# Heads and low-rank products by turns on the rows of the array, in a hybrid RWKV / retention / SSD / attention trunk

## The chip, the cores and the metric

The kernel runs on one core of a Trainium2 chip. The metric is device microseconds of that core for one execution of the whole program.

## The reference

Two layers (DEPTH = 2) of one trunk are applied to 128 context tokens and 512 latent tokens, width 1024, all in float32. Each layer norms its input, projects it into four groups of 256 channels (RWKV-7, retention, a state-space scan, differential attention), puts the four outputs through one projection, and then runs a gated convolutional feed-forward. The parts that the change touches are, in RWKV, the low-rank decay and gate, and in retention, the scores inside a chunk:

```
wd = wd.reshape(b, t, 2, 32); ad = ad.reshape(b, t, 2, 32)
w_lora = einsum('btdr,drc->btdc', tanh(wd), rwkv_w_up)
decay = exp(-exp(-softplus(-(rwkv_w0 + w_lora)) - 0.5))
a = sigmoid(rwkv_a0 + einsum('btdr,drc->btdc', ad, rwkv_a_up))
# RWKV state, per head of 64, both directions
S = S diag(w) + S (-kk)^T (kk * a) + v^T k;  o = S r
# retention, per head of 64 and chunk of 128
scores = einsum('bihd,bjhd->bijh', qc, kc) * decay
y = einsum('bijh,bjhe->bihe', scores, vc) + (qc * exp(cum)) S
```

## The kernel before

Channels lie on the partitions and tokens on the free axis: 512 latent columns, a zero column, 128 context columns (T = 642, STREAMS). All products are issued through one helper, mm, at line 84, so that the trace shows that line for nearly all of them and the tile names tell them apart. A product in plain float32 shows in the trace as two matmul records. Dense projections split their operands into two float32r parts and make three products each.

A Tile scheduler orders the instructions of an engine: an instruction that is ready early may stand ahead of one that comes earlier in the program, and program order is the priority among ready ones. PSUM is in two halves. The right one holds two pairs of banks for dense products. The left one (sbank, given out by SMT and XMT, in turn) holds four single banks during the RWKV scans, and three plus one for the modulation during retention.

**RWKV.** Each layer has four scans: two tiles t of two heads (64 channels each), two directions d. Scan i + 1 is prepared (rw_pre) beside the substitution of scan i (rw_sub) and the solve of scan i - 1 (the generator behind); the loops pump these generators a yield at a time, and the dense projections fill the rest. In rw_pre the inner function lora (line 524) makes tw, the decay, and ta, the gate: wa holds 128 rows, 32 for each of decay and gate in each direction. The weight tile wl [128, 4, 256] has in block g only the 32 rows of group g and zeros elsewhere, so that a product over all 128 rows picks one group. One call makes the products of 512 and of 128 columns (ztw or zta, line 530) with a Tanh on ACT behind each (line 532); tw is made whole, then ta. DVE then sums the decays (cum, line 550), and kd, AR and BK follow. The scores (sc) are made in three groups of 4, 4 and 2 chunks of 64 tokens (lines 590 to 597): for head 0 a bank is taken, 4 products of 64 rows are made and DVE multiplies the result by two masks (sca, pk); then the same for head 1. The substitution (xox, GU, xo) and the solve (bg, y, gq, st) take the same four banks.

**Retention.** It runs in an outer loop with the state-space scans, the modulation of what comes later (mps) and the projections that are left; each round takes one step of retention and of the state-space scans, 0.75 of modulation_behind and 0.5 of left(), whose last step is the value projection of the attention, dv (RS = (0.5, 0.0, 0.75, 1, 1, 1, 0.5)). The generator retention yields after kt and vw, then after each head (scores rsc into pt, in groups of 4 chunks and 1; qd on POOL), after three state steps (rin), after rin_c, after ryl and ryc with the squares, and in head_out (hs_ret, the statistics, and R_ret, their spread). The output goes to DRAM and is loaded again for the output projection. Two tiles t run one after the other.

**Derived.** Once a layer, wl is cleared on POOL (line 1312) and filled by four DMAs issued by ACT (line 1314).

Of the kernel before, what the change touches and what calls it, by code (L numbers as in the profile page):

```python
# [23 lines left out]
# token columns: latents 0..511, a zero column, context 513..640, a zero column  # L24
# [18 lines left out]
# columns of the per-layer parameter block  # L43
# [10 lines left out]
# columns of the constant block  # L54
# [17 lines left out]
def tile_trunk(ctx: ExitStack, tc: tile.TileContext, xT, cT, wmod, win, wv1, wv2, wout, wup, wdn, wlora, gup, pp, srw,  # L72
# [13 lines left out]
    class Pool:  # L86
        """A tile pool that can be closed out of turn; `bufs` per tag."""
# [14 lines left out]
    class Banks:  # L102
        """A half of PSUM: two pairs of banks (for the dense products) or four single banks."""
# [26 lines left out]
    def XMT(name):  # L130
        """a bank beside the dense products"""
        return sbank.tile(name)

# [23 lines left out]
    # silu(c) = u * (1 + tanh(u)), u = c / 2  # L157
# [30 lines left out]
    def w_pair(src, name):  # L188
        """the two halves (four blocks of the contraction each) of one column tile"""
        return [w_split(src[i], 512, f"{name}_{i}") for i in range(2)]  # L190
# [18 lines left out]
    def modulation(l, qs, bank=SMT, burst=False, pool=None):  # L209
        """in steps: one for each tile of weights, or (burst) for four of them"""  # L210
# [23 lines left out]
    def modulation_blocks(blocks, pool, n):  # L234
        """whole blocks, n tiles of weights loaded ahead"""
# [35 lines left out]
    def modulation_behind(l, qs, bank, pool, after):  # L271
        """loads, products and sums a step apart, each behind what runs beside it"""
# [42 lines left out]
    def spread(r, n, name, d, bank=SMT):  # L315
        """r [128 tokens, 5 * n]: rows of channels; n = 1 for all 128 channels, 2 for two heads of 64."""
# [12 lines left out]
    def x_stats(x, xp, name):  # L329
        """1/rms of x per token, spread over the partitions."""  # L330
# [21 lines left out]
    def norm(l, which, x, xp, name, before=None):  # L352
        """the stream h = rmsnorm(x) * g * (1 + scale) + shift, in two parts, zero columns between the streams"""
# [33 lines left out]
    def cm_product(parts, h, name, M=128):  # L387
        """[M channels, 2 halves of the tokens with one column of overlap on each side]"""
        hhi, hlo = h
        ps = MMT(name)  # L390
        for k in range(KD):
            wh, wl = wk(parts, k, M)
            for w_, r_, a, b in ((wh, hhi, k == 0, False), (wh, hlo, False, False), (wl, hhi, False, k == KD - 1)):
                for j, p0 in ((0, 0), (1, 321)):
                    mm(ps[:M, j, 0:324], lhsT=w_, rhs=r_[:, k, p0:p0 + 324], start=a, stop=b)
        return ps
# [4 lines left out]
    def tok_product(l, src, n, h, name, dest):  # L401
        """token rows of h @ W: dest [128 tokens, 5, n]"""
# [19 lines left out]
    def conv(ps, out, wl, wc, wr, bias=None, M=128):  # L422
        """centred taps along the tokens, from PSUM"""
# [10 lines left out]
    def head_stats(sqs, n, name, floor=None, scale=1.0 / 64, eps=EPS, bank=SMT, tg=""):  # L434
        """sqs: channel tiles [128, T] of squares -> per token and head, 1/sqrt, [128 tokens, 5 * n * len(sqs)]"""
# [8 lines left out]
    # mixer inputs and outputs wait in DRAM for their turn  # L444
# [18 lines left out]
    # ================= RWKV-7 =================  # L463
# [7 lines left out]
    def rw_proj(l, h, key, dv, out):  # L471
        """one projected tile, tokens shifted"""
# [11 lines left out]
    def rw_prep(l, t, f, dv, rw):  # L484
        """half normalised keys, and the values with tokens on partitions"""
# [10 lines left out]
    def rw_values(l, t, f, rw):  # L496
        """values with tokens on partitions: even chunks of 64 in the upper half, odd ones in the lower"""
# [18 lines left out]
    def rw_pre(l, t, d, f, wa, rw, dv, S, need):  # L516
        """up to the scores inside chunks and the right-hand sides"""
# [7 lines left out]
        def lora(base, bias, tag):  # L525
            out = RT(tag)[:, 0:T]
            pads(out)
            for c0, n in STREAMS:
                z = SMT(f"z{tag}{nm}_{c0}")
                mm(z[:, 0:n], lhsT=dv["wl"][:, base // 32, t * 128:t * 128 + 128], rhs=wa[:, c0:c0 + n],  # L530
                   start=True, stop=True)
                act(out[:, c0:c0 + n], z[:, 0:n], AF.Tanh, bias=dv[bias][:, td:td + 1], scale=0.5)
            return out

        tw = lora(32 * d, "w0h", "tw")
        ta = lora(64 + 32 * d, "a0h", "ta")
        yield
        # log decays, summed inside chunks of 64 with a leading (trailing) zero
# [40 lines left out]
        # scores inside chunks of 64, transposed: rows (b | k) of token j, columns (a | r) of token i  # L579
# [5 lines left out]
        for g, ms in enumerate(GRP):  # L585
# [4 lines left out]
            for h in range(2):  # L590
                ps = SMT(f"sc{nm}_{g}_{h}")
                for e in range(nb):
                    mm(ps[:, 128 * e:128 * e + 128], lhsT=B2[64 * h:64 * h + 64, n0 + e, :],
                       rhs=A4[64 * h:64 * h + 64, :, n0 + e, :], start=True, stop=True)
                p4 = ps[:, 0:128 * nb].rearrange("p (e s c) -> p e s c", e=nb, s=2)
                vtt(sca[:, h, n0:n0 + nb], p4[:, :, 0, :], maskA.unsqueeze(1).to_broadcast([128, nb, 64]), MULT)
                vtt(pk[:, 0:nb, h, 1, :], p4[:, :, 1, :], maskR.unsqueeze(1).to_broadcast([128, nb, 64]), MULT)
            # the strict blocks of 32 on the diagonal
# [12 lines left out]
        def rhs():  # L611
# [4 lines left out]
            for g, ms in enumerate(GRP):  # L616
# [7 lines left out]
                # right-hand sides [a | A_ak v], tokens on partitions, two chunks a pack  # L624
# [15 lines left out]
    def rw_sub(l, t, d, rw, dv, S):  # L640
        """inverses of the 16-blocks of I - A, transposed, by substitution"""
# [19 lines left out]
        # combined to blocks of 32: X1 O X2 beside the diagonal (X2 O X1 backwards)  # L661
# [21 lines left out]
        # and to blocks of 64: what lies beside the diagonal of the inverses is X1 O X2 again  # L683
# [6 lines left out]
        for e in range(2):  # L690
            # empty in this direction
# [24 lines left out]
    def rw_solve(l, t, d, f, rw, dv, y, S):  # L716
        """solve, the chunk maps, the states from chunk to chunk, the outputs"""
# [47 lines left out]
        # states from chunk to chunk; MI = [state (key, value) ; identity]  # L765
# [37 lines left out]
    def rw_end(l, t, f, rw, dv, y):  # L803
# [5 lines left out]
        # group norm over each head  # L809
# [19 lines left out]
    # ================= projections that wait =================  # L829
    def rope_tile(ps, out, tab, sp, nm):  # L830
        """rotary pairs lie 16 partitions apart in every 32; context columns turn by 0"""
# [8 lines left out]
    def silu2(ps, o):  # L840
        """2 * silu, from PSUM"""
# [43 lines left out]
    def diff_proj(l, h, sp):  # L885
        tab = sp.tile([128, 2, 660], tag="tab", name=f"dtab{l}")
        nc.scalar.dma_start(tab[:, :, 0:T], rope[1])
        # queries and keys in two exact parts, the cache behind the keys of the tokens
# [23 lines left out]
    def tokens_to_partitions(dst, src, nm):  # L912
        """dst [128 tokens, 5, 128] from src [128 channels, T]"""
# [6 lines left out]
    def head_out(l, nm, kk, y, sq, gcol, gate, bank=XMT, eps=EPS):  # L920
        """sq: the squares of y, then room"""
# [16 lines left out]
    # ================= retention =================  # L938
    def retention(l, t, mp, tokv, dv):
# [6 lines left out]
        # states entering each latent chunk: rows 0-63 forward, 64-127 backward  # L946
# [13 lines left out]
        # scores inside chunks of 128, transposed, times the decay of both directions  # L960
        pts, qds = [], []
        for h in range(2):
            rows = slice(64 * h, 64 * h + 64)
            pt = mp.tile([128, 5, 128], tag="pt", name=f"rpt{nm}_{h}")
            for n0, n1 in ((0, 4), (4, 5)):
                ps = XMT(f"rsc{nm}_{h}_{n0}")
                for n in range(n0, n1):
                    mm(ps[:, 128 * (n - n0):128 * (n - n0) + 128], lhsT=k[rows, TOK[n]:TOK[n] + 128],
                       rhs=q[rows, TOK[n]:TOK[n] + 128], start=True, stop=True)
                vtt(pt[:, n0:n1], ps[:, 0:128 * (n1 - n0)].rearrange("p (n i) -> p n i", i=128),  # L970
                    D4[:, h, t].unsqueeze(1).to_broadcast([128, n1 - n0, 128]), MULT)
            qd = mp.tile([128, 4, 128], tag="qd", name=f"qd{nm}_{h}")
# [3 lines left out]
            pts.append(pt)  # L976
            qds.append(qd)
            yield
# [40 lines left out]
    # ================= state-space duality =================  # L1019
    def ssd_dt(l, dtr, dv):  # L1020
        """dt = softplus, with log1p(e) = 2 atanh(e / (2 + e)); the decays that follow from it"""
# [24 lines left out]
        # sums of g: after j (forward) and before j (backward), and over the whole chunk  # L1046
# [854 lines left out]
```

## Time and profile before

| what | value |
|---|---|
| runs | 2264.86, 2267.35, 2267.46 us; median 2267.35 us |
| span of the profiled execution | 2266.46 us |
| PE, DVE, ACT, POOL busy | 94%, 58%, 36%, 12% |
| layer 0, RWKV scans | about 84 to 300 us |
| layer 0, retention | about 370 to 500 us |
| the same stages of layer 1 | some 1117 us later |

The profile is of one execution. PE is the engine of the matmuls, DVE the vector engine, ACT the scalar engine, POOL the third elementwise engine; the queues that issue DMAs are shown as SPq, ACTq, POOLq. A name such as ztw is the tile written; "ztw<-wa,wl" gives the tile and what it reads; a shape such as 32*128 128x512 is rows times columns of the array, then the output. Records of a pipelined matmul overlap, so the time from one start to the next start is what a product takes of PE, not its own duration. PEclk is the granted clock as a share of the full one.

### The profile page before, as it was taken

The numbers are of one execution on the slowest core, as the hardware profiler recorded it, in microseconds if no ns is written. First come the engines' busy times: TensorE is split into PE (matmuls) and PEld (weight loads), VectorE is DVE, ScalarE is ACT, GpSimd is POOL, SyncE is SP. The second block draws the span as 40 slices with busy tenths as digits, with TensorE's granted clock in tenths as the row PEclk, the third lists the DMA queues.
The fourth block names the chain that finished last, engine by engine and source line by source line (L and its number), as shares of the span: only waits on it lengthen the run. The fifth ranks groups of instructions, "written<-read, shape, count | busy, mean of one in ns | idle before, by whom it ended". The sixth has DMA issues, their size and how long they took to land. (4 is left out here: it accounts for less than half of the span.)

```text
span 2266.5 us, 41011 instructions
## 1 busy us (share of the span) xinstructions
PE 2136.9 (94%) x16265; PEld 1936.7 (85%) x16265; DVE 1307.2 (58%) x2951; ACT 816.4 (36%) x1603; POOL 275.2 (12%) x468
## 2 busy tenths in 40 slices
PE   6999999979999999999989999999799999999997
PEld 3887887767878899999988888777678899999997
DVE  3687776547564435545457777755475654454553
ACT  4343432226343313323344334332363432232332
POOL 3111122210020000000031111222001100000002
PEclk9999999988989999999999999999799999999998
DMA  6212126575233332222332211365832222222221
GB/s 241 77 55 67 49 80 226 181 213 137 68 94 121 123 87 71 71 79 75 92 89 60 72 51 56 98 221 176 235 102 73 75 75 71 75 73 77 73 72 67
DMA packets 130943, 232.26 MB, mean 102 GB/s; under 512 B 14784, under 2 KB 34752, under 8 KB 130752
## 3 DMA queue, kind: packets, MB, share of 16 engines
q1 hardware_dynamic: 98304, 176.47, 26.4%
q10 hardware_dynamic: 32448, 53.17, 7.2%
q8 instruction: 129, 2.11, 0.4%
q14 instruction: 62, 0.51, 0.1%
HBM read 199.16 MB, written 30.42 MB: 101 GB/s over the span
## 5 line engine op out<-in xcount | busy, mean ns | idle before, releaser
L84 PE MATMUL pu<-hhi_n,wh_up 128*128 128x324 f32 x1408 | 326.9, 314 | 0.6 <-DVE gv L426 0.6
L84 PE MATMUL pu<-hlo_n,wh_up 128*128 128x324 f32 x1408 | 325.9, 313 | 0.5 <-POOL hlo_n L381 0.4
L84 PE MATMUL pu<-hhi_n,wl_up 128*128 128x324 f32 x1408 | 324.5, 312 | 0.0
L185 DVE TENSOR_TENSOR wl_up<-wr_up,wh_up 128x512 fp32r<-128x512 f32 x176 | 123.2, 706 | 236.2 <-ACT wh_up L184 232.5
L84 PEld LDWEIGHTS pu<-hhi_n,wh_up 128*128 128x128 f32 x1408 | 238.1, 190 | 16.1 <-issue 10.0
L84 PEld LDWEIGHTS pu<-hlo_n,wh_up 128*128 128x128 f32 x1408 | 239.5, 190 | 1.9 <-issue 0.8
L84 PEld LDWEIGHTS pu<-hhi_n,wl_up 128*128 128x128 f32 x1408 | 239.3, 190 | 0.0
L184 ACT CAST wh_up<-wr_up 128x512 fp32r<-128x512 f32 x176 | 108.3, 617 | 291.4 <-issue 136.5
L84 PE MATMUL pd<-gh,wh_dn 128*128 128x322 f32 x704 | 162.5, 312 | 0.0
L84 PE MATMUL pd<-gh,wl_dn 128*128 128x322 f32 x704 | 162.4, 312 | 0.0
L84 PE MATMUL pd<-gl,wh_dn 128*128 128x322 f32 x704 | 162.3, 312 | 0.0
L184 ACT CAST wh_dn<-wr_dn 128x512 fp32r<-128x512 f32 x96 | 56.0, 584 | 207.4 <-PE pd L84 148.2
L185 DVE TENSOR_TENSOR wl_dn<-wr_dn,wh_dn 128x512 fp32r<-128x512 f32 x96 | 61.9, 646 | 106.7 <-ACT wh_dn L184 105.9
L84 PEld LDWEIGHTS pd<-gh,wh_dn 128*128 128x128 f32 x704 | 119.6, 190 | 0.8 <-ACT wh_dn L184 0.8
L84 PEld LDWEIGHTS pd<-gl,wh_dn 128*128 128x128 f32 x704 | 119.3, 190 | 0.5
L84 PEld LDWEIGHTS pd<-gh,wl_dn 128*128 128x128 f32 x704 | 119.2, 190 | 0.0
L432 DVE SCALAR_TENSOR_TENSOR x<-pd,mod,x 128x322 f32<-128x322 f32 x144 | 54.5, 434 | 92.4 <-PE pd L84 92.4
L425 DVE SCALAR_TENSOR_TENSOR gv<-pu,pp,gv 128x642 f32<-128x642 f32 x88 | 78.0, 887 | 41.2 <-ACT gv L424 34.8
L84 PE MATMUL po<-ohi,wh_out 128*128 128x320 f32 (+1 forms) x256 | 79.1, 333 | 14.8 <-ACT ohi L199 14.4
L424 ACT ACTIVATE gv<-pu,pp 128x642 f32<-128x642 f32 x88 | 77.8, 884 | 39.0 <-PE pu L84 39.0
L84 PE MATMUL mps<-wr_mod,sc 128*32 128x512 f32 x384 | 77.3, 672 | 2.9 <-DMA wr_mod<-in_wmod 2.9
L426 DVE SCALAR_TENSOR_TENSOR gv<-pu,pp,gv 128x642 f32<-128x642 f32 x88 | 78.0, 886 | 3.1
(742 smaller groups left out, 4521.9 us busy)
## 6 DMA issues: line engine op xcount, KB each, us to landing
wr_mod<-in_wmod SPq DMA_DIRECT2D x192, 256.0 KB, 4.1
wr_up<-in_wup SPq DMA_DIRECT2D x176, 256.0 KB, 2.6
wr_dn<-in_wdn SPq DMA_DIRECT2D x64, 256.0 KB, 2.7
wr_dn<-in_wdn SPq DMA_DIRECT2D x32, 192.0 KB, 2.4
olo<-scr_o ACTq DMA_DIRECT2D x16, 321.0 KB, 4.6
wr_out<-in_wout SPq DMA_DIRECT2D x16, 256.0 KB, 2.6
wr_out<-in_wout SPq DMA_DIRECT2D x32, 128.0 KB, 2.1
x_in<-in_xT SPq DMA_DIRECT2D x8, 321.0 KB, 5.9
```

Source lines behind the costliest of these rows:

```text
L84: last_pe = nc.tensor.matmul(*a, **k).ins
L184: nc.scalar.copy(hi[:, :n], raw[:, :n])
L185: vtt(lo[:, :n], raw[:, :n], hi[:, :n].bitcast(F32), SUB)
L424: act(v2(out), ps[:M, :, 1:322], AF.Identity, bias=0.0 if bias is None else bias, scale=wc)
L425: vstt(v2(out), ps[:M, :, 0:321], wl, v2(out), MULT, ADD)
L426: vstt(v2(out), ps[:M, :, 2:323], wr, v2(out), MULT, ADD)
L432: vstt(xs, halves[j][:, o:o + n], g[:, s:s + 1], xs, MULT, ADD)
```

## The change

- rw_pre: lora is gone. tw and ta are both taken; for each stream of columns the decay product and the gate product are issued one after the other, each on its own 32 rows of wa and wl (base 32 d and 64 + 32 d), into two banks; then the two Tanh follow.
- rw_pre, scores: in each group the banks of both heads are taken first, the products go by turns (head 0, head 1), and then DVE masks head 0 and head 1.
- retention: both pt tiles are taken; in each group of chunks both heads' banks are taken, the products go by turns, DVE multiplies, and the generator yields; then the qd of both heads, and a yield. That is three yields a tile where there were two.
- derived: wl is [128, 256] and is filled by one DMA; the clearing on POOL is gone.

The core of the diff (the rest removes comments and docstrings):

```
-        def lora(base, bias, tag):
-            out = RT(tag)[:, 0:T]
-            pads(out)
-            for c0, n in STREAMS:
+        tw, ta = RT("tw")[:, 0:T], RT("ta")[:, 0:T]
+        pads(tw)
+        pads(ta)
+        for c0, n in STREAMS:
+            zs = []
+            for base, tag in ((32 * d, "tw"), (64 + 32 * d, "ta")):
                 z = SMT(f"z{tag}{nm}_{c0}")
-                mm(z[:, 0:n], lhsT=dv["wl"][:, base // 32, t * 128:t * 128 + 128], rhs=wa[:, c0:c0 + n],
-                   start=True, stop=True)
+                zs.append(z)
+                mm(z[:, 0:n], lhsT=dv["wl"][base:base + 32, t * 128:t * 128 + 128], rhs=wa[base:base + 32, c0:c0 + n],
+                   start=True, stop=True, tile_position=(base, 0))
+            for z, out, bias in zip(zs, (tw, ta), ("w0h", "a0h")):
                 act(out[:, c0:c0 + n], z[:, 0:n], AF.Tanh, bias=dv[bias][:, td:td + 1], scale=0.5)
-            return out
-
-        tw = lora(32 * d, "w0h", "tw")
-        ta = lora(64 + 32 * d, "a0h", "ta")
         yield
...
-            for h in range(2):
-                ps = SMT(f"sc{nm}_{g}_{h}")
-                for e in range(nb):
+            pss = [SMT(f"sc{nm}_{g}_{h}") for h in range(2)]
+            for e in range(nb):
+                for h, ps in enumerate(pss):
                     mm(ps[:, 128 * e:128 * e + 128], lhsT=B2[64 * h:64 * h + 64, n0 + e, :],
                        rhs=A4[64 * h:64 * h + 64, :, n0 + e, :], start=True, stop=True)
+            for h, ps in enumerate(pss):
                 p4 = ps[:, 0:128 * nb].rearrange("p (e s c) -> p e s c", e=nb, s=2)
...
         for h in range(2):
-            rows = slice(64 * h, 64 * h + 64)
-            pt = mp.tile([128, 5, 128], tag="pt", name=f"rpt{nm}_{h}")
-            for n0, n1 in ((0, 4), (4, 5)):
-                ps = XMT(f"rsc{nm}_{h}_{n0}")
-                for n in range(n0, n1):
+            pts.append(mp.tile([128, 5, 128], tag="pt", name=f"rpt{nm}_{h}"))
+        for n0, n1 in ((0, 4), (4, 5)):
+            pss = [XMT(f"rsc{nm}_{h}_{n0}") for h in range(2)]
+            for n in range(n0, n1):
+                for h, ps in enumerate(pss):
+                    rows = slice(64 * h, 64 * h + 64)
                     mm(ps[:, 128 * (n - n0):128 * (n - n0) + 128], lhsT=k[rows, TOK[n]:TOK[n] + 128],
                        rhs=q[rows, TOK[n]:TOK[n] + 128], start=True, stop=True)
-                vtt(pt[:, n0:n1], ps[:, 0:128 * (n1 - n0)].rearrange("p (n i) -> p n i", i=128),
+            for h, ps in enumerate(pss):
+                vtt(pts[h][:, n0:n1], ps[:, 0:128 * (n1 - n0)].rearrange("p (n i) -> p n i", i=128),
                     D4[:, h, t].unsqueeze(1).to_broadcast([128, n1 - n0, 128]), MULT)
+            yield
+        for h in range(2):
+            rows = slice(64 * h, 64 * h + 64)
             qd = mp.tile([128, 4, 128], tag="qd", name=f"qd{nm}_{h}")
...
-            pts.append(pt)
             qds.append(qd)
-            yield
+        yield
...
-        dv["wl"] = rw.tile([128, 4, 256], F32, tag="wl", name=f"wl{l}")
-        nc.gpsimd.memset(dv["wl"], 0.0)
-        for g in range(4):
-            nc.scalar.dma_start(dv["wl"][32 * g:32 * g + 32, g], wlora[l, 32 * g:32 * g + 32])
+        dv["wl"] = rw.tile([128, 256], F32, tag="wl", name=f"wl{l}")
+        nc.scalar.dma_start(dv["wl"], wlora[l])
```

## Rows read from the trace of the kernel before

**Rows 1.** The page, part 1: busy time of each engine.

```profile
PE 2136.9 (94%) x16265; PEld 1936.7 (85%) x16265; DVE 1307.2 (58%) x2951; ACT 816.4 (36%) x1603; POOL 275.2 (12%) x468
```

**Rows 2.** Table by stage: stretch, length, busy by engine, PEclk, DMA share, GB/s.

```profile
84.00:300.00 216.00, 208.09 (x2430) 179.87 (x2430) 169.09 (x565) 85.91 (x183) 34.39 (x110) 0.96 0.21 62
```

**Rows 3.** Timeline of PE, stage's end: start, us, operation, count [idle before, releaser].

```profile
482.88 0.39 PE L84 MATMUL dv<-wh_dv,hhi_n 128*128 128x256 f32 x1
...
491.38 0.28 PE L84 MATMUL dv<-wh_dv,hlo_n 128*128 128x256 f32 x1
491.60 0.45 PE L84 MATMUL ryl<-rpt,tokv 128*64 128x128 f32 x4
...
493.70 1.05 PE L84 MATMUL mps<-cs,macc 128*128 128x2 f32 x8
495.34 1.67 PE L84 MATMUL hs_ret<-cs,rsq 128*128 128x2 f32 x10 [0.58 <-ACT rsq L1015]
```

**Rows 4.** Timeline of PE, first scan of layer 0.

```profile
84.33 1.24 PE L84 MATMUL ztw<-wa,wl 128*128 128x512 f32 x4
85.40 1.25 PE L84 MATMUL zta<-wa,wl 128*128 128x512 f32 x4
86.40 0.39 PE L84 MATMUL p0gd<-hlo_n,wh_in0gd 128*64 128x324 f32 x1
```

**Rows 5.** Timeline of PE, scores of the first and the second scan.

```profile
92.95 3.60 PE L84 MATMUL sc<-AR,BK 64*128 64x128 f32 x40 [0.75 <-DVE BK L569]
...
137.64 1.16 PE L84 MATMUL sc<-AR,BK 64*128 64x128 f32 x8
138.73 0.39 PE L84 MATMUL rv<-wl_rv,hhi_n 128*128 128x264 f32 x1
...
139.41 1.16 PE L84 MATMUL sc<-AR,BK 64*128 64x128 f32 x8
...
146.62 0.72 PE L84 MATMUL sc<-AR,BK 64*128 64x128 f32 x8
147.28 0.45 PE L84 MATMUL st<-MI,gq 128*64 128x64 f32 x4
```

**Rows 6.** Timeline of PE, third scan of layer 1.

```profile
1296.68 2.00 PE L84 MATMUL zta<-wa,wl 128*128 128x512 f32 x4
1298.61 0.82 PE L84 MATMUL xo<-G,XO 32*32 32x32 f32 x40
```

**Rows 7.** Timeline of PE, retention scores of the first tile, layer 0.

```profile
383.17 1.38 PE L84 MATMUL rsc<-ldrq,ldrk 64*128 64x128 f32 x10
384.48 1.06 PE L84 MATMUL mps<-wr_mod,sc 128*32 128x512 f32 x6
```

**Rows 8.** Timeline of ACT, first scan.

```profile
85.38 0.95 ACT L532 ACTIVATE tw<-ztw,d_w0h 128x512 f32<-128x512 f32 x2 [0.74 <-PE ztw L84]
```

**Rows 9.** Timeline of DVE, second scan's decays.

```profile
123.22 0.51 DVE L686 STREAM_TRANSPOSE GU<-G 128x320 f32<-128x320 f32 x1
...
125.54 1.51 DVE L550 TENSOR_TENSOR_SCAN cum<-rmask,lw 128x650 f32<-128x650 bf16 x1
127.09 0.48 DVE L712 COPY XO<-xo 32x320 f32<-32x320 f32 x1
```

**Rows 10.** Timeline of PE, xo in the second and the fourth scan.

```profile
125.03 0.82 PE L84 MATMUL xo<-GU,sca 32*32 32x32 f32 x40
...
240.93 0.76 PE L84 MATMUL xo<-GU,sca 32*32 32x32 f32 x36
```

**Rows 11.** Timeline of DVE, masks of the first scan; gq in the second.

```profile
94.33 0.40 DVE L596 TENSOR_TENSOR sca<-sc,cs 128x256 f32<-128x256 f32 x1
...
138.46 0.57 DVE L754 TENSOR_TENSOR gq<-bg,AR 64x128 f32<-64x128 f32 x2
```

**Rows 12.** Tile wl: operation, count: ns min/median/max, first and last start.

```profile
L1314 ACTq DMA_DIRECT2D wl<-in_wlora x8: 317/432/532, 55.6 to 1177.8; - x8
L1312 POOL MEMSET wl<- x2: 945/953/961, 53.6 to 1174.4; 128x1024 f32 x2
```

## The prediction

> **What bounds the kernel now.** I read the page first: over the span of 2266.46 us PE is busy for 94% [rows 1]. The median of the runs shown, 2267.35 us, is 0.89 us above this span; the sum below is made against the span, and the 0.89 is added at the end. The change touches only the mixer stages, so next I read the table by stage: from 84 to 300 us, where the four RWKV scans of layer 0 run, PE is busy for 208.1 of 216.0 us and DVE for 169.1 [rows 2]. Layer 1 repeats all of it some 1117 us later. PE executes in the order written, and dense products (p0gd, rv, p0z and others) fill the places between the small products of the scans; so a microsecond of PE time that goes away lets the dense products end earlier, unless the next small product then waits for DVE or ACT. At the end of the stage this is plain: the value projection dv runs without a gap to 491.4 us, and only behind it come the outputs of the second retention tile, ryl, its statistics hs_ret and all that follows [rows 3]. What PE saves before is therefore passed on to the end, and what comes late into that tail is paid there.
>
> **Part 1, the decay and gate products** (ztw, zta; line 530 before). Each of the eight scans has a tw product and a ta product for 512 and for 128 columns, each shown as two records. In the first scan tw takes 85.40 - 84.33 = 1.07 us and ta 86.40 - 85.40 = 1.00 us [rows 4]. After the change they use 32 different rows each and stand in the order tw, ta, tw, ta. Whether such products run beside each other is seen at the scores: the two heads of the last group, on different 64 rows, take 0.66 us for 8 records (146.62 to 147.28) where one head alone takes 1.09 us for 8 (137.64 to 138.73) [rows 5]. So a pair costs about as much as one, and up to 1.00 us a scan goes, in the block at 1294 us, which runs at half the pace, 1.93 us [rows 6]. No row has 32-row products of 512 columns; the bounds are the whole overlap and none. A change of row layout costs about 0.1 us: ten rsc records take 1.31 us and eight sc records 1.09 us, so a record costs 0.11 and 0.2 us is left for the way in and out [rows 5, 7]. The products now have the 128 rows of their dense neighbours; six such changes are added in all (two each in the first scans, one each in the last ones), 0.6 us. The Trainium skill, "TensorEngine Tiling (Array Packing)", section "Tiling Modes", speaks against the edit here: a change of the tiling mode drains the engine. The rows agree that it costs something, and put it at the 0.1 us above.
>
> What of this lies on the path differs by place.
> - First scans (84, 1201): dense p0gd and p1gd follow. 1.00 - 0.2 = 0.8 is freed, but ACT now does ta's 512 columns ahead of tw's last 128; the two activations of tw take 0.95 together [rows 8], the larger of ta's, some 0.6, comes in between, and the decay sum waits that much longer. I take 0.4 each: 0.8.
> - Scans of 122 and 1239: GU is ready at 123.22 + 0.51 = 123.73 [rows 9], but PE reaches xo only at 125.03 [rows 10], so the whole 1.0 is a gain for xo. Then DVE copies XO only behind the sum cum, which ends at 125.54 + 1.51 = 127.05 [rows 9], and cum comes later as before. I take 0.7 each: 1.4.
> - Scans of 179 and 1294: xo waits in the same way; 1.0 and 1.9 freed, I take 0.9 and 1.7: 2.6.
> - Scans of 238 and 1357: the next xo starts at 240.93 [rows 10] and waits for a DVE transpose, so most is lost; 0.3 each: 0.6.
>
> Sum 5.4 us; bounds 8.6 (all of it) and -4.8 (no overlap, 0.6 for the changes, and the 0.6 of ACT in seven scans).
>
> **Part 2, the RWKV scores** (sc). The two first scans already run 40 records in 3.60 us, 0.09 apiece, the heads overlapped; the twelve DVE masks of the result, 0.40 us each and one behind the other from 94.33 on, set the pace [rows 5, 11]: zero. In the six others the second head starts later: it runs at 139.41, dense rv stands between [rows 5], because its bank was still read by DVE's gq, which ends at 138.46 + 0.57 = 139.03 [rows 11]. Fourteen head pairs are like that, four are paired already. Giving out both banks first doesn't free the second one sooner; the order of instructions follows what is ready, so I expect head 0, dense, head 1 as before: zero. Were both free at once, a group of 16 records would take 0.66 + 4 x 0.11 = 1.10 us and not 2 x 1.09; twelve such and two smaller (0.6) give 14.2 us.
>
> **Part 3, the retention scores** (rsc). Eight runs of ten records, 1.31 us for one [rows 7]. Paired, sixteen and four records take 1.10 + 0.43 us, 1.1 less a tile, four tiles, 4.4 us. There are three banks here, shared with the state-space scan, so often one head will start alone; I take 0.5 a tile, 2.0 us (bounds 0 and 4.4).
>
> The same edit makes three yields of two in each tile. A round of the outer loop does one step of retention, 0.75 of the modulation, half a step of the projections. Counting steps, ryl of the second tile goes from round 18 to 20; the modulation ends in round 19, and the value projection is written in round 16. So the last modulation products, 1.05 us at 493.70, now in the gap in which PE waits for ACT's squares (hs_ret, 0.58 idle) [rows 3], come ahead of ryl, and the state steps of the second tile fall behind dv. Queued behind: ryl, hs_ret, the store and load of that output, the output projection. I take one such block a layer, 1.1, twice: -2.2 us. Bounds: 0, and 5 a layer if the three state steps wait for all of dv.
>
> **Part 4, the weights wl.** Two memsets of 0.95 us on POOL and six of eight DMA issues of 0.43 us on ACT go [rows 12], SP's queue isn't touched. Dense p0v and p0r cover them: 0, at most 1.2 gained. The smaller tile wl and the moved pads and qd products on POOL change no work.
>
> **Sum.** 5.4 + 0 + 2.0 - 2.2 + 0 = 5.2 us. 2266.46 - 5.2 = 2261.26, and with 0.89 this is 2262.15, say 2262.2 us.
>
> **Rivals.**
> A. Nothing is left: the PE time freed in the scans turns into waits for DVE. For it: DVE is busy for 78% of the stage [rows 2] and cum and the ACT order get later. Against: xo waits for PE alone at four places. Time: 5.4 and 2.0 shrink to the 2.2 that the tail costs, 2267.4.
> B. The scores pair too: 14.2 more, 2248.0. Against it speaks the bank of [rows 11].
> C. Slower: the two added retention rounds decide. From the point at which two or more state steps of the second tile find dv ahead of them, the tail starts some 5 us later in each layer: 2267.35 - 7.4 + 10 = 2270, or 2272 with part 1 half absorbed. For it: dv is unbroken for 9 us and the tail has no other work.
> D. Slower too: both banks are claimed and the order does alternate, so that head 1's first product waits for its bank on PE with the rest of head 0 and the dense work behind it. The price is the dense work between the heads, 139.41 - 138.73 = 0.68 us [rows 5], at fourteen places 9.5 us: 2271.7. The Trainium skill, "TensorE: Matmul & The Clock Gate", Part 3, says that matmuls keep program order in start and end; the records above start in one order too. By that rule nothing could pass a waiting product.
>
> **How the numbers follow.** The forecast has 0.48; inside it the time lies between 2254 (part 1 and 3 whole, tail free) and 2267. A 0.20, B 0.08, C 0.18, D 0.06. What a measurement of this kernel can tell from no change is about 0.2%, 4.5 us, so faster is below 2262.8 and slower above 2271.9. Faster: 0.35 of the forecast and B, 0.43. Same: 0.13 of the forecast, A, 0.06 of C and D: 0.39. Slower: the rest of C and D, 0.18. The range leaves out B and the ends of C and D: 2253 to 2272.5.
>
> **What would show it.** Right: ztw and zta take some 1.3 us a scan, not 2.1, their records start in pairs, xo at the places of 122 and 179 starts about 1 us sooner after xox; sc looks as before in six scans. Part 3: rsc in runs of 16 and 4. Wrong: a group of sc in 1.1 us (B), a stall within sc (D), rin of the second tile behind dv (C), and new idle time ahead of xo (A).

## The result and the profile after

The changed kernel takes 2288.82 us (median of 6 runs, 2278.05 to 2297.62) where the one before takes 2267.4 us in the same comparison (2257.12 to 2269.36): a ratio of 1.012, 95% interval 1.0093 to 1.0146 (the two medians alone give 1.0094). A second measurement (e7_whole below) gave 2286.16 us and 1.0112 (1.008 to 1.0144). The forecast was 2262.2 us, range 2253.0 to 2272.5: the sign is wrong and the time lies outside the range.

First the page, part 1, of the kernel after, and the views of the cores (span, mean granted clock) of before and of after:

```profile
PE 2155.7 (94%) x16265; PEld 1952.8 (85%) x16265; DVE 1311.3 (57%) x2951; ACT 813.9 (35%) x1603; POOL 279.4 (12%) x466
```

```profile
core 0: 2266.5 us, clock 0.963
```

```profile
core 0: 2295.0 us, clock 0.948
```

Against [rows 1] PE has as many instructions and is busy 18.8 us longer, and its idle time grew from 2266.5 - 2136.9 = 129.6 to 2295.0 - 2155.7 = 139.3 us. The pairs take less of PE than before (next), and yet PE is busy longer: more of it runs at the lower clock. The clock records of the traces hold two levels alone, full and half, so the mean clock gives the time at half clock as 2 x span x (1 - clock): 168 us before, 239 us after.

The pairs themselves are as hoped in the first scans. The timeline of PE in the first scan, after (start us, us, operation; it answers [rows 4]):

```profile
84.38 0.69 PE L84 MATMUL ztw<-wa,wl 32*128 32x512 f32 x1
84.39 0.69 PE L84 MATMUL zta<-wa,wl 32*128 32x512 f32 x1
...
85.45 0.27 PE L84 MATMUL ztw<-wa,wl 32*128 32x128 f32 x1
85.46 0.27 PE L84 MATMUL zta<-wa,wl 32*128 32x128 f32 x1
85.66 0.36 PE L84 MATMUL p0gd<-hlo_n,wh_in0gd 128*64 128x324 f32 x1
```

The block takes 85.66 - 84.38 = 1.28 us, where before it took 86.40 - 84.33 = 2.07 us. But look at the fourth scan. First its stretch of 20 us in the table by stage (columns as in [rows 2]; the granted clock is the third number from the end), before and then after; behind it the timeline of PE after, which answers the second line of [rows 10]:

```profile
236.00:256.00 20.00, 19.47 (x317) 16.81 (x306) 16.91 (x38) 10.49 (x20) 3.31 (x8) 1.00 0.13 45
```

```profile
236.00:256.00 20.00, 19.06 (x317) 17.10 (x316) 13.68 (x31) 8.90 (x18) 1.26 (x4) 0.74 0.15 44
```

```profile
238.05 0.46 PE L84 MATMUL p0sx<-hlo_n,wh_in0sx 128*128 128x324 f32 x2
238.35 0.31 PE L84 MATMUL p0sx<-hhi_n,wl_in0sx 128*128 128x324 f32 x1
238.59 0.86 PE L84 MATMUL xox<-OX,GT 32*32 32x16 f32 x80
239.38 0.69 PE L84 MATMUL ztw<-wa,wl 32*128 32x512 f32 x1
...
240.46 0.27 PE L84 MATMUL zta<-wa,wl 32*128 32x128 f32 x1
241.67 1.06 PE L84 MATMUL xo<-GU,sca 32*32 32x32 f32 x40 [0.94 <-ACT tw L537]
242.66 0.64 PE L84 MATMUL p0sx<-hhi_n,wl_in0sx 128*128 128x324 f32 x1
243.10 0.74 PE L84 MATMUL p0sx<-hhi_n,wh_in0sx 128*128 128x324 f32 x2
```

Two things are new. xo waits 0.94 us for ACT's tw: by the code the two pairs hold all four banks, and xo needs one of them. The Trainium skill, "TensorEngine Tiling (Array Packing)", section "Restrictions and Gotchas", warns that row tiling raises the pressure on PSUM; this wait is such a case. And from about 242 us PE is at half clock: two p0sx records took 0.46 us at 238.05 and take 0.74 at 243.10. What PE did before the clock fell is in the lines: small xox, the four products on 32 rows, a wait, and xo, some 4 us without one dense product. Before, the padded products stand there and the stretch is at 1.00.

### The profile page after: what moved, and what is told of

Same layout as the page of the kernel before. It is cut to its first block, busy times and chain, and to the rows that moved or that the text cites. A ratio compares the mean times of both kernels' runs of the same rounds, so it can differ in the third digit from the quotient of the medians.

```text
span 2295.0 us, 40965 instructions
## 1 busy us (share of the span) xinstructions
PE 2155.7 (94%) x16265; PEld 1952.8 (85%) x16265; DVE 1311.3 (57%) x2951; ACT 813.9 (35%) x1603; POOL 279.4 (12%) x466
## 5 line engine op out<-in xcount | busy, mean ns | idle before, releaser
L425 DVE SCALAR_TENSOR_TENSOR gv<-pu,pp,gv 128x642 f32<-128x642 f32 x88 | 78.0, 887 | 42.7 <-ACT gv L424 36.2
L84 PE MATMUL po<-ohi,wh_out 128*128 128x322 f32 (+1 forms) x256 | 79.3, 333 | 0.6 <-DVE x L432 0.4
L84 PE MATMUL po<-olo,wh_out 128*128 128x322 f32 (+1 forms) x256 | 79.5, 331 | 0.4 <-DVE olo L200 0.4
```

Of the source, the lines that this page charges most:

```text
L84: last_pe = nc.tensor.matmul(*a, **k).ins
L425: vstt(v2(out), ps[:M, :, 0:321], wl, v2(out), MULT, ADD)
```

## The experiments

Kernels measured together ran on one chip and share its runs of before, whose medians were 2263.2 us (for e1 to e4), 2261.5 (e5 to e9), 2263.5 (e10 to e13) and 2261.4 (e14 to e16). Across these four groups, compare the ratios, or the distance from a kernel's own runs of before, and not the times. "Half clock" in the tables is worked out as above for every timed run; the median of a kernel's runs is given (149 to 154 us for before). "Written order" is the order in which the compiled program lists the instructions of an engine. One figure of it is used below: how many dense products (modulation and the projections of 128 channels, as trace records) stand ahead of the first sums of the state-space scan in layer 0, 880 before and 913 after.

### The parts alone

**e1_lora**: parts 1 and 4 alone, exactly the first and the last block of the diff shown above.

> Only parts 1 and 4 (32-row products by turns, one load of wl). Theory CLOCK: what PE saves is work that kept the granted clock up; beside the xox and xo of the fourth scan the clock falls, some 10 us of half clock in each layer (242 to 252 us and its like in layer 1), as in the profile of the whole change. Time 2262 from the work plus 6 from the clock, about 2268, half-clock time 20 us above the 168 us of before. Theory TAIL (the loss sits in the retention rounds): the clock is as before and the time is the forecast of part 1, 2262. Either way the pairs start together and a scan's block takes 1.3 to 1.9 us where PE doesn't wait.

2306.05 us, ratio 1.02 (1.017 to 1.0231), half clock 224 us. CLOCK had the direction; neither had the size. This part alone loses 43 us, more than the whole change (21 to 25).

**e2_scores**: part 2 alone, exactly the second block of the diff.

> Only part 2 (RWKV scores by turns, both banks first). Both theories: nothing, 2267 within 3; six scans keep head 0, dense products, head 1. If it is slower by more than 5, the forecast's zero was wrong and the loss sits in the order of the scores: the first scans' 40 records took 4.19 us in the whole change against 3.58 before.

2271.66 us, 1.0054 (1.003 to 1.0078), half clock 164 us. The zero was wrong by some 8 us. In the first scan PE now stops inside the scores. Timeline of PE, e2_scores, against the first line of [rows 5]:

```profile
93.64 2.06 PE L84 MATMUL sc<-AR,BK 64*128 64x128 f32 x32 [0.74 <-DVE BK L569]
96.51 0.46 PE L84 MATMUL sc<-AR,BK 64*128 64x128 f32 x2 [0.81 <-DVE pk L598]
97.17 0.68 PE L84 MATMUL sc<-AR,BK 64*128 64x128 f32 x6 [0.21 <-DVE pk L598]
97.84 0.41 PE L502 MATMUL vt<-cs,rwv 128*128 128x128 f32 x2
```

The third group waits for its banks, and 40 records take 97.84 - 93.64 = 4.2 us instead of 3.6. In the other scans head 0, dense, head 1 stayed.

**e3_ret** and **e16_ret3**: part 3 alone, the same kernel twice (the retention block of the diff shown above).

> Only part 3 (retention scores by turns, three yields). Theory TAIL: the second tile's state steps and all behind them come a round or two later, 2272 to 2278, with half-clock time within 10 us of the 168 us of before. Theory CLOCK: the retention stages get 40 to 50 us of new half clock (about 375 to 392, 440 to 447 and the like in layer 1), and that costs some 15 us: 2278 to 2282. If it stays below 2270 the loss of the whole change isn't in retention by itself.

2259.37 us, 0.9992 (0.9969 to 1.0015), half clock 160 us. TAIL and CLOCK both fall.

> Part 3 alone with its three yields, on the same chip and beside the same runs of before. If three yields gain over two (2266.8, ratio 1.0015): ratio to before 0.997 to 0.9995. If the first measurement (0.9992) was the chip's: 1.000 to 1.002. The prediction's tail rival would want it 3 to 5 us above before.

2254.24 us, 0.9977 (0.9954 to 1.0), half clock 156 us. Part 3 costs nothing that can be seen, and its medians lie 4 and 7 us below before. Of all kernels here it has the lowest time; its interval just touches no change, so a gain is not shown.

**e13_ret2**: part 3 with two yields.

```
                     D4[:, h, t].unsqueeze(1).to_broadcast([128, n1 - n0, 128]), MULT)
-            yield
+            if n0 == 0:
+                yield
```

> Part 3 alone with two yields a tile, as before (the queries' decay stays in the step of the last chunk). If the extra yield costs what the prediction put there (1.1 us a layer), 2 us faster than part 3 with three yields: ratio to before 0.998. If the extra yield is free, the same as part 3: 0.999. Half-clock time 150 to 165 us.

2266.84 us, 1.0015 (0.9996 to 1.0034). Not faster than with three: the added yield, to which the prediction gave 2.2 us of loss, costs nothing that can be seen. Whether it gains stays open: the two were on the same chip but not in the same comparison, and their intervals overlap.

### Order against rows

By now the loss lay in part 1, and part 1 does two things: it uses 32 rows, and it writes the four products in another sequence. The scheduler plans by shapes that don't show the rows, so kernels that differ in the rows alone come out with the same written order on PE. That gives pairs. What still goes with the rows is the tile wl: the padded kernels keep its clearing and its four DMAs (part 4).

**e4_padded**: the whole change, on 128 rows with the padded weights of before.

```
-                mm(z[:, 0:n], lhsT=dv["wl"][base:base + 32, t * 128:t * 128 + 128], rhs=wa[base:base + 32, c0:c0 + n],
-                   start=True, stop=True, tile_position=(base, 0))
+                mm(z[:, 0:n], lhsT=dv["wl"][:, base // 32, t * 128:t * 128 + 128], rhs=wa[:, c0:c0 + n],
+                   start=True, stop=True)
```

> The whole change, but the decay and gate products keep all 128 rows with the zero-padded weights of before (their new order, decay and gate by turns, stays). Theory CLOCK, with the rows as its cause: the half clock at 242 to 252, 1252 to 1263 and 1372 to 1382 us goes, 30 us of it, and the time is some 9 us below that of the whole change, 2274 to 2280, although PE has 4 us more to do. Theory TAIL: no better than the whole change, 2283 to 2292.

2279.07 us, 1.0083 (1.0057 to 1.0109), half clock 178 us against 215 in the second measurement of the whole change. As CLOCK said; but 16 of the whole change's 25 us remain on 128 rows.

**e5_lorapad**: the same edit on e1_lora, so part 1's turns on 128 rows and nothing else.

> Part 1 alone but with all 128 rows and the padded weights: decay and gate by turns, nothing else. The order of PE's instructions is exactly that of part 1 alone (2306.05), the rows are those of before. Theory ORDER: the turns make the scheduler put dense products ahead of the small ones of the scans (577 dense rows ahead of the second scan's ox where before there were 543, 809 ahead of the second bn where there were 753), and that costs the time: 2290 to 2306, more than half of the 43 us of part 1 alone. Theory ROWS: the 32 rows cost the time through the clock; with 128 rows it is 2260 to 2270.

2296.54 us, 1.0154 (1.0129 to 1.0179), half clock 197 us: within what ORDER said.

**e6_rows**: the kernel before with 32 rows and the small wl, decay whole and then gate as before.

```
-                mm(z[:, 0:n], lhsT=dv["wl"][:, base // 32, t * 128:t * 128 + 128], rhs=wa[:, c0:c0 + n],
-                   start=True, stop=True)
+                mm(z[:, 0:n], lhsT=dv["wl"][base:base + 32, t * 128:t * 128 + 128], rhs=wa[base:base + 32, c0:c0 + n],
+                   start=True, stop=True, tile_position=(base, 0))
```

> Only the rows of part 1: both products on their own 32 rows with the small wl, but decay whole and then gate, so that PE's order is exactly that of before. Theory ORDER: 2258 to 2266, as before. Theory ROWS: the clock falls behind the 32-row products, 2275 to 2295.

2271.49 us, 1.0039 (1.0023 to 1.0056), half clock 182 us. The time lies between the two statements: with the order unchanged the rows alone cost 9 to 10 us. With e5_lorapad, both theories hold, each for its share.

**e7_whole**: the whole change again.

> The whole change once more, with a second profile. Both theories: 2278 to 2298, as in the first runs. If PE's order sets the time, idle time and the delays of sums and rsc against before stay as in the first profile (sums about -0.3 and +18.6 us, rsc +9.5 us), while the stretches at half clock move.

2286.16 us, 1.0112 (1.008 to 1.0144), half clock 215 us. The half-clock stretches did move; the delays stayed about as they were (sums +2.0 and +22.8 us, rsc +9.6).

**e9_rows_ret**: e6_rows and part 3, the edit just shown and the retention block of the diff.

> The 32 rows in the old order and the whole of part 3; scores of RWKV as before. A try at what is left if the order of the scans isn't touched. Theory ORDER: as part 3 alone, 2252 to 2262, at or below before. Theory ROWS: slower than part 3 alone by 10 or more, 2270 to 2290.

2263.23 us, 1.001 (0.9992 to 1.0028), half clock 179 us: 8 us below e6_rows, level with before, and 1 us above what ORDER said.

### The order given back

The four products can be written in other sequences. This one puts 877 dense products ahead of the first sums: decay of the context first, then decay and gate of the latents side by side, then the gate of the context.

**e10_va**: part 1 with that sequence.

```
-            zs = []
-            for base, tag in ((32 * d, "tw"), (64 + 32 * d, "ta")):
...
-            for z, out, bias in zip(zs, (tw, ta), ("w0h", "a0h")):
...
+        zw1 = one(*W_, 1)
+        fin(tw, "w0h", 1, zw1)
+        zw0 = one(*W_, 0)
+        za0 = one(*A_, 0)
+        fin(tw, "w0h", 0, zw0)
+        fin(ta, "a0h", 0, za0)
+        za1 = one(*A_, 1)
+        fin(ta, "a0h", 1, za1)
```

Here one(...) makes the product of a group (W_ decay, A_ gate) and a stream (0 latents, 1 context) on its 32 rows, and fin(...) its Tanh.

> Part 1 alone with another sequence: decay of the 128 context columns first, then decay and gate of the 512 latent columns side by side, then the gate of the context. The large pair still overlaps, but the decay is whole before the gate's second product, and the written order of PE goes back to nearly that of before: 877 dense products ahead of the sums of the state-space scan (before 880, part 1 alone 928). Theory ORDER AND ROWS: the 35 us of the order go, the 10 us of the rows' clock stay, the overlap gives up to 4 back: 2266 to 2273, half-clock time 175 to 190 us. Theory PAIRS (what costs is that two banks are claimed and two products run at once): 2290 to 2306, as part 1 alone.

2273.05 us, 1.0043 (1.0019 to 1.0067), half clock 182 us. 33 us of part 1's 43 are gone (10 above its runs of before) with nothing but another sequence of the same four products and their Tanhs, the large pair still side by side. PAIRS falls.

**e11_va_ret**: e10_va's edit and part 3, the retention block of the diff.

> The same sequence of part 1 with part 3 (retention by turns, three yields). ORDER AND ROWS: part 3 gave 3 to 8 us, so 2258 to 2267, level with before. PAIRS: 2282 to 2300.

2270.04 us, 1.0025 (1.0002 to 1.0048), half clock 193 us; above the stated 2267, the half clock is higher than in e10_va.

**e12_va_whole**: the whole change with e10_va's sequence, that is e10_va's edit and the blocks of parts 2 and 3.

> The whole change with that sequence of part 1: dense products ahead of sums 904, as with the scores by turns alone, against 913 in the whole change and 880 before. ORDER AND ROWS: 2262 + 10 for the scores' order + 10 for the rows - 5 for part 3 = 2277, 2270 to 2281, below the whole change (2286). PAIRS: 2284 to 2292, no different from the whole change.

2271.93 us, 1.0031 (1.0011 to 1.0051), half clock 188 us: 8 us above its runs of before, where the whole change was 25 above.

**e14_va128** and **e15_va_whole128**: the tenth and the twelfth again on 128 rows (the edit of e4_padded in one(...)), with the same written order each.

> The sequence of the tenth run (context decay first, then the large pair, then the context gate), but over all 128 rows with the padded weights; PE's order is exactly that of the tenth run. If the 10 us that stayed there are the rows' effect on the clock: 2258 to 2266, half-clock time 140 to 165 us. If they are what is left of the changed order: 2268 to 2276, half clock 175 to 190 us.

2268.43 us, 1.0029 (1.001 to 1.0048), half clock 161 us: the half clock is as one statement had it, the time as the other. By the ratios about a third of what e10_va lost (0.0014 of 0.0043) is the rows and two thirds a rest of the order; the two intervals overlap, so the split is not clear of noise.

> The whole change with that sequence and 128 rows; PE's order is that of the twelfth run (2271.9). Rows: 8 to 10 us below it, 2260 to 2266, half clock 155 to 170 us. Order: 2268 to 2276.

2263.04 us, 1.0008 (0.9985 to 1.0031), half clock 161 us: by the ratios most of what was left (0.0023 of 0.0031) is the rows.

### What they say together

Each line has one written order on PE; the columns differ only in the rows and the tile wl. As only the first pair was measured side by side, the difference is that of the ratios, times 2262 us:

| written order | 128 rows: us, ratio (half clock) | 32 rows: us, ratio (half clock) | difference, us |
|---|---|---|---|
| of before | 2261.5, 1 (149) | 2271.5, 1.0039 (182) | 8.8 |
| decay and gate by turns | 2296.5, 1.0154 (197) | 2306.1, 1.02 (224) | 10.4 |
| e10_va's sequence | 2268.4, 1.0029 (161) | 2273.1, 1.0043 (182) | 3.2 |
| whole change | 2279.1, 1.0083 (178) | 2286.2, 1.0112 (215) | 6.6 |
| whole with e10_va's sequence | 2263.0, 1.0008 (161) | 2271.9, 1.0031 (188) | 5.2 |

**The rows** cost 3 to 10 us in all five, although the 32-row block is the shorter one. The first pair shows it beyond noise; in the others the intervals overlap, and it is the same sign five times that speaks. Every time the half clock grows by 21 to 37 us with it. Within one kernel, from run to run, a microsecond more at half clock goes with 0.3 to 0.5 us more time (kernels with 10 or more runs, and the runs of before); at that rate 33 us of half clock cost 10 to 16 us, which covers the whole difference. That rate is a correlation: no run changed the clock and nothing else. Timelines of PE in the second scan, e5_lorapad and then e1_lora, which have the same order, at the same rv products behind the four products:

```profile
128.51 0.29 PE L84 MATMUL rv<-wh_rv,hhi_n 128*128 128x264 f32 x1
```

```profile
127.83 0.28 PE L84 MATMUL rv<-wh_rv,hhi_n 128*128 128x264 f32 x1
...
128.32 0.42 PE L84 MATMUL rv<-wh_rv,hhi_n 128*128 128x264 f32 x1
```

In the second kernel the clock falls at 128 us and the record goes from 0.28 to 0.42 us; in the first it stays at 0.29. It is not so in every kernel: in the kernel after, with 32 rows too, it stays at this place (below).

**The order** costs 35 us on 128 rows (2261.5 to 2296.5), the larger share. The timelines of DVE in the second scan show how; they answer [rows 9]. First e5_lorapad, then e10_va:

```profile
126.32 0.43 DVE L546 TENSOR_SCALAR lw<-tw 128x512 f32<-128x512 f32 x1 [1.21 <-ACT tw L536]
127.27 0.48 DVE L713 COPY XO<-xo 32x320 f32<-32x320 f32 x1 [0.53 <-PE xo L84]
127.79 0.23 DVE L546 TENSOR_SCALAR lw<-tw 128x128 f32<-128x128 f32 x1
127.93 0.70 DVE L185 TENSOR_TENSOR wl_rv<-wr_rv,wh_rv 128x528 fp32r<-128x528 f32 x1
128.55 1.50 DVE L551 TENSOR_TENSOR_SCAN cum<-rmask,lw 128x650 f32<-128x650 bf16 x1
```

```profile
124.69 0.19 DVE L557 TENSOR_SCALAR lw<-tw 128x128 f32<-128x128 f32 x1
126.28 0.43 DVE L557 TENSOR_SCALAR lw<-tw 128x512 f32<-128x512 f32 x1 [1.41 <-ACT tw L538]
126.74 1.51 DVE L562 TENSOR_TENSOR_SCAN cum<-rmask,lw 128x650 f32<-128x650 bf16 x1
128.29 0.48 DVE L724 COPY XO<-xo 32x320 f32<-32x320 f32 x1
```

By turns, the decay is whole only after the gate's large product, and the scheduler writes the copy of XO and the split of a dense weight ahead of the decay sum cum. Counted from the start of xox in each kernel (121.89 before, 123.26 in e5_lorapad, 122.91 in e10_va), cum starts after 3.65, 5.29 and 3.83 us. The account that fits the rest is argued, not shown: the scheduler writes dense products into the time that the scan seems to need (928 ahead of the first sums), and these are missing where they had covered small products later. Timing of a dense projection: shortest, median and longest duration in ns, first and last start, from the views of the tile p0sB; before first, then e5_lorapad:

```profile
L84 PE MATMUL p0sB<-hhi_n,wl_in0sB x16: 307/313/417, 264.4 to 282.1; 128*128 128x324 f32 x16
```

```profile
L84 PE MATMUL p0sB<-hhi_n,wl_in0sB x16: 308/314/414, 242.4 to 257.3; 128*128 128x324 f32 x16
```

The dense p0sB is done 25 us sooner. Where the time goes shows in the stage from the first sums of the state-space scan to the first retention scores (rsc), in layer 0 and in layer 1. Table by stage, before first, then e5_lorapad:

```profile
305.40:371.80 66.40, 62.19 (x451) 53.48 (x450) 46.67 (x120) 22.27 (x53) 23.70 (x24) 1.00 0.36 124
1420.90:1489.70 68.80, 63.79 (x451) 54.94 (x450) 47.81 (x121) 22.46 (x53) 23.75 (x24) 0.98 0.41 135
```

```profile
307.80:386.80 79.00, 68.93 (x446) 56.39 (x446) 50.09 (x127) 22.24 (x54) 21.25 (x23) 0.91 0.39 126
1435.10:1514.80 79.70, 69.65 (x457) 58.33 (x456) 45.81 (x118) 22.12 (x54) 20.83 (x23) 0.92 0.36 120
```

The sums come 2.4 us later in layer 0 and 14.2 us later in layer 1 (layer 0's lag included), and the stage takes 12.6 and 10.9 us more, together 23.5, and the whole profiled executions differ by 22.4 (2288.9 and 2266.5). PE is idle there for 10 us a layer where it was for 4 to 5, and the granted clock is 0.91 and 0.92 where it was 1.00 and 0.98.

Over the whole span PE's idle time is 2288.9 - 2145.8 = 143.1 us against 129.6 before, and half clock is 48 us longer at the median, 14 to 24 us by the rate above. So of the 35 us about 14 are idle time and the rest may be the clock. That split is worked out, not measured by a run of its own.

The number of dense products ahead of the sums is no measure of the loss: e15_va_whole128 has 904 and is level with before, e2_scores has 904 too and is 8 us slower, e14_va128 has 877 and is 7 us slower. Which part of a changed order costs is not shown; that the turns cost it, and that another sequence gives most of it back, is.

## Why the prediction was wrong, point by point

- **What bounds the kernel.** PE at 94%, right. The sentence that failed is the next one: "a microsecond of PE time that goes away lets the dense products end earlier, unless the next small product then waits". It holds the written order fixed. The order isn't what is ready on the chip; it is planned as a whole ahead of it: in the compiled programs at least 1290 of PE's 13417 products stand elsewhere by the turns alone, and on the same 128 rows that order takes 35 us more. The prediction itself said that PE executes in the order written, and then moved single products as if the rest stayed.
- **Part 1, the size of the pair.** "A pair costs about as much as one" is right: 1.28 us a block in the first scans, 0.8 less, as in the sum. In the fourth scan the block with the wait takes 241.67 - 239.38 = 2.29 us, no less than before (2.18): the wait for a bank wasn't in the sum. Of the sign named for the gain, xo about 1 us sooner, 0.5 us came at the place of 179 (1.90 us behind the first ztw, 2.36 before) and nothing at that of 122 (3.63 us behind xox, 3.14 before).
- **Part 1, the decay sum.** The prediction saw that ta comes ahead of tw's last 128 columns and charged 0.1 to 0.4 us a scan, with 0.6 as the bound. Measured from xox it is 5.27 - 3.65 = 1.6 us in the second scan after the change (cum starts at 128.57, xox at 123.30). This is the mis-sized term, and its direct price is the small part of it. With the decay whole first (e10_va) it is 0.2 us, and 28 to 33 us of the loss go with it, on 128 and on 32 rows; that the one brings the other through the scheduler's plan is argued from this, not shown by itself.
- **Part 1, the clock.** The prediction gave the products' price at full clock and used the half clock only for the block at 1294 us. That the clock of what follows could fall when the padding goes was not in it, a term put at nothing; e6_rows measures 33 us more at half clock and 9 to 10 us more time. Its bounds (8.6 gained to 4.8 lost; its own terms give 7 x 1.00 + 1.93 - 0.6 = 8.3 for the first) therefore left out both terms that decided; measured, part 1 loses 43 us.
- **Part 2.** "Head 0, dense, head 1 as before" is right for the scans behind the first ones, and the reason given, the bank under gq, fits: in e2_scores too the second head starts at 141.22, behind gq, which ends at 140.26 + 0.57 = 140.83. The zero is not: 8 us, of which the stall in the first scans is 0.6 us in each layer. The rest came with the new written order; how much is clock and how much idle time was not separated. On top of e10_va's sequence parts 2 and 3 together cost nothing (7 us above before in e14_va128, 2 in e15_va_whole128); even if part 3 gives its 4 to 7 us there, part 2 costs 2 us at most (an estimate), so the 8 us are no price of the scores as such.
- **Part 3.** Near the forecast: 0.2 us of loss were forecast (2.0 gained, 2.2 lost), 4 and 7 us of gain measured at the medians. The modulation products did move ahead of most of ryl, and the gap before hs_ret grew. Timeline of PE after, against [rows 3]:

```profile
498.35 1.05 PE L84 MATMUL mps<-cs,macc 128*128 128x2 f32 x8 [0.51 <-DVE macc L289]
499.33 0.32 PE L84 MATMUL ryl<-qd,rst 128*64 128x128 f32 x1
...
504.08 1.62 PE L84 MATMUL hs_ret<-cs,rsq 128*128 128x2 f32 x10 [2.57 <-ACT rsq L1021]
```

  2.57 us idle there, 0.58 before, and 1.92 in e3_ret. Yet part 3 alone isn't slower.
- **Part 4.** Zero fits: the small wl is in e6_rows, whose whole loss the half clock would cover at the rate above.
- **The rivals.** A (absorbed) names the waits but not the loss. B did not come. C, the retention tail, was given as the way to lose and is not it: part 3 alone is even. Its sign did come, its price did not. Timeline of PE, e3_ret, the end of dv in layer 0 (before, the last rin starts at 474.0 and dv's last product, in [rows 3], at 491.4):

```profile
488.54 0.28 PE L84 MATMUL dv<-wh_dv,hlo_n 128*128 128x256 f32 x1
488.75 0.68 PE L84 MATMUL rin<-vw,kt 128*64 128x64 f32 x8
```

  State steps (rin) of the second tile do stand behind dv, but dv ends sooner: from the first rsc to the last hs_ret the two layers together take 248.1 us in e3_ret and 245.5 in e16_ret3, against 245.5 before. With two yields (e13_ret2) no rin is behind dv, and it is not faster.

  D has the right mechanism, head 1 waiting on PE for a bank, but in the first scans and at 0.6 us. The case that came, another written order and a lower clock, had no chance of its own.
- **The sum.** The parts don't add: 43 + 8 - 4 = 47 us alone, 21 to 25 together. Each edit gives the scheduler another plan, and what one edit costs depends on the others: with e10_va's sequence on 128 rows the same parts 2 and 3 leave the kernel level with before.

## What to carry to other kernels

Where a scheduler writes the instruction order, look at the order that a change gives before pricing its products; here another sequence of the same four small products was worth 33 us. Products that are padded to more rows of the array need not be pure waste: here their replacement by products on fewer rows went with 21 to 37 us more at half clock in five pairs. And where two products use different rows, it was enough here to write them near each other; turns weren't needed for the overlap (below), and cost the order.

## What the runs showed of the hardware

**Products on other rows don't wait their turn.** In e6_rows PE's written order is decay of 512 columns, decay of 128, gate of 512, gate of 128. Its timeline of PE in the first scan:

```profile
84.66 0.69 PE L84 MATMUL ztw<-wa,wl 32*128 32x512 f32 x1
84.67 0.69 PE L84 MATMUL zta<-wa,wl 32*128 32x512 f32 x1
...
85.62 0.27 PE L84 MATMUL ztw<-wa,wl 32*128 32x128 f32 x1
...
85.94 0.36 PE L84 MATMUL p0gd<-hlo_n,wh_in0gd 128*64 128x324 f32 x1
```

The gate's large product starts at 84.67, 0.95 us ahead of the decay's small one at 85.62, which is written before it, and the block takes 1.28 us, as by turns. The Trainium skill, "TensorE: Matmul & The Clock Gate", Part 3, says that matmuls keep program order in start and end; these rows differ, and the measurement decides.

**A busy PE can lose its clock.** The table by stage of the second scan's stretch, before and then e6_rows, which has the same written order; behind them the kernel after and e10_va, which have 32 rows and other orders:

```profile
118.00:138.00 20.00, 19.00 (x347) 16.61 (x346) 16.60 (x39) 9.38 (x18) 1.96 (x5) 1.00 0.32 96
```

```profile
118.00:138.00 20.00, 18.71 (x328) 16.81 (x327) 16.17 (x37) 7.71 (x16) 1.83 (x4) 0.83 0.27 79
```

```profile
118.00:138.00 20.00, 19.10 (x351) 17.02 (x350) 16.79 (x43) 9.61 (x19) 5.99 (x4) 1.00 0.31 96
118.00:138.00 20.00, 18.04 (x345) 16.26 (x344) 16.95 (x41) 8.93 (x17) 1.83 (x4) 1.00 0.28 91
```

PE is busy for 19.00 and 18.71 of 20 us in the first two, and the granted clock is 1.00 and 0.83. The Trainium skill, "TensorE: Matmul & The Clock Gate", Part 1, lets the gate follow how busy PE has been; the busy time alone doesn't tell these apart, as e10_va kept 1.00 with 18.04. What differs between the first two is that two products on 128 rows became two on 32 that run at once, with a short wait behind them. The 32 rows alone don't decide a given stretch either, as the last two lines show. Over a whole kernel the half clock grew with the 32 rows in all five pairs; which of the three the clock answers to, no run here separates.
